# Respacing the hand-written order of an encoder layer's token mixer on one Trainium2 core

## The chip, the core and the metric

One core of one Trainium2 chip runs the whole layer as one program. The metric is the device time of one execution in microseconds (us); the median of several runs is compared. Engines are named as in the profile: PE (matmul), PEld (its weight loads), DVE (VectorE), ACT (ScalarE), POOL (GpSimd), SP (SyncE, which here only issues DMAs).

## What is computed

An encoder layer of 256 tokens with 1024 channels, all in float32:

```python
y = token_mixer(x)             # dilated-window attention (8 heads) and differential attention (4 heads),
                               # merged by sigmoid gates, then one output projection
x = layer_norm(alpha * x + y)
y = moe_ffn(x)                 # 32 experts, the 4 largest router logits of a token
x = layer_norm(alpha * x + y)

merged = sigmoid(g_a) * (o_a @ w_proj_a) + sigmoid(g_b) * (o_b @ w_proj_b)
token_mixer = merged @ w_out + b_out
expert(xb) = clamped_swiglu(xb @ w_up[e] + b_up[e]) @ w_down[e] + b_down[e]
```

## The kernel before

**Two halves.** The mixer (lines 131 to 700) reads 28 slabs of weights of 1 MB each (`w_mix`), the experts' half (784 to 959) reads 384 tiles of 1 MB each (`w_ex`, 12 for each expert). Expert tiles go through 20 named places in on-chip memory (`SLOTS`, line 81); the mixer uses the same places for its own data, and an expert tile can be fetched into a place as soon as the mixer's last use of it is over. `load()` (115) issues the next tile; the order of places is a0, qa, qb, tab, v, pt, p, gbc, oa, ob, ga, bup, gb, s0, s1, s2, w0, w1, x0, x1. All these DMAs go out on SP, which works through its list in order: a DMA that must wait for its place holds up those behind it.

**Pieces.** The mixer's matmuls go by 112 pieces of 512 columns, four in a slab. Float32 weights are split into a high and a low half: `split(n)` (176) lets ACT round the high half, and DVE or POOL subtract it to give the low half (line 187; POOL takes pieces 1 and 3 of a slab, except in slabs 2, 3, 8 and 9, which DVE does by line 184). The halves lie in a ring of four pieces (places w0, w1), so a split runs at most some three pieces ahead of PE. After the last split of a slab, its place is refilled with the slab three further on. `next_piece(n)` (199) first runs the hooks set for piece n-1, then `split(n+3)`; the caller then issues the matmuls of piece n, six or eight of them (lines 216 to 230).

**The order by hand.** `at(n, f)` (196) puts step f ahead of piece n+1. All engines run their own list in this order, with no scheduler. Lines 506 to 529 set it: attention A (dilated) for four head pairs as `tables_a`, `scores`, `scaled_a`, `turned_a`, `values_a`; attention B (differential) for four heads as the same steps with `_b`; `squares_b` and `subln_b` (its norm); `gate_sigmoids` (456); `bias_loads` and eight `bias_part` (432 to 448), in which POOL cuts the experts' up bias into three bfloat16 parts stacked in 96 rows (`bupp`), six or seven operations at a time; `residual_in` (453), alpha * x + b_out on DVE, from `x_loads`; `router_parts` (467), which folds the norm's gain into the router's weights through PE and DVE; and the `load`s. Units of 4 or 8 pieces follow one another (530): values, queries and keys of A are pieces 0 to 23, of B 24 to 47, gates 48 to 79, the two projections 80 to 95, the output projection 96 to 111. A unit ends with its results being read from PSUM by ACT or DVE (263 to 274); `n` in `unit(n)` times four is its first piece.

**The end of the mixer** (656 to 697) does the last quarter of the output projection for token tile 0, then 1 (`quarter(tt, i)`), with norm, transposes (`turned_x`), router logits and the choice of experts (`largest`) among them. Then the first expert's tokens are gathered (716) and its first matmuls run (742), which begin to set places free.

## Time and profile before

| | us |
|---|---|
| median of 3 runs (1165.01 to 1166.2) | 1166.2 |
| the profiled execution | 1164.82 |
| its span, first to last instruction | 1163.1 |
| PE busy | 1088.7 |
| DVE busy | 264.6 |
| ACT busy | 244.2 |
| POOL busy | 109.7 |

A busy PE is one with a matmul in flight; matmuls overlap, so a busy PE is not PE at its peak. In the timeline a row gives start, duration, engine, line, operation, written<-read tiles and count, and in brackets the idle time of the engine before it and the instruction that ended it. HBM traffic is 438 MB, of which the experts' tiles are 403 MB.

### The profile page before, as it was taken

How to read it: one execution, taken by the hardware profiler on the slowest of the kernel's cores; microseconds unless marked ns; L12 is line 12 of the kernel's file. 1: busy time of each engine (PE TensorE's matmuls, PEld its weight loads, DVE VectorE, ACT ScalarE, POOL GpSimd, SP SyncE). 2: the span in 40 equal slices, each digit the busy share in tenths (PEclk: the TensorE clock that was granted, in tenths of full speed). 3: DMA queues.
4: the chain of work that ended last, by engine and by line, in shares of the span. 5: the costliest groups of instructions: out<-in, count | busy, mean ns of one | idle time of the engine just before them, and what ended most of it. 6: DMA issues, size and time to landing. Idle time of an engine off the chain costs nothing.

```text
span 1163.1 us, 13105 instructions
## 1 busy us (share of the span) xinstructions
PE 1088.7 (94%) x5295; PEld 482.5 (41%) x5296; DVE 264.6 (23%) x512; ACT 244.2 (21%) x517; POOL 109.7 (9%) x114
## 2 busy tenths in 40 slices
PE   7999979899999999999999989999999899999994
PEld 6777758633434333333333323343433332323231
DVE  5675647311111111111111101111111111010113
ACT  5766644411111111111111101010111010101010
POOL 1535666000000000000000000000000000000000
PEclk9999999899999999999999989999999999999997
DMA  9663667799999999999999999999999999999992
GB/s 342 237 208 110 242 243 304 301 413 422 421 421 421 422 420 421 421 421 421 421 421 421 422 421 422 422 421 422 421 421 422 421 421 420 421 421 421 422 420 107
DMA packets 63542, 440.14 MB, mean 378 GB/s; under 512 B 7283, under 2 KB 8947, under 8 KB 10772
## 3 DMA queue, kind: packets, MB, share of 16 engines
q1 hardware_dynamic: 63138, 438.81, 92.1%
q8 instruction: 44, 0.72, 0.3%
q10 hardware_dynamic: 338, 0.43, 0.1%
q14 instruction: 22, 0.18, 0.0%
HBM read 438.17 MB, written 1.05 MB: 378 GB/s over the span
## 4 chain that ended last, share of the span: by engine, by line
DMA 54%; PE 37%; DVE 3%; POOL 2%; ACT 2%; issue 1%; SPq 0%; ACTq 0%; POOLq 0%; DVEq 0%
DMA r_ob<-in_w_ex 13%; DMA r_w<-in_w_ex 12%; DMA r_qa<-in_w_ex 12%; DMA r_s<-in_w_ex 9%; PE pu L742 8%; DMA r_pt<-in_w_ex 7%; PE pg L742 6%; PE pd L774 5%; PE acc L782 2%; PE px L716 2%; PE pt L219 2%; PE pt L229 2%; PE pt L230 1%; PE pt L228 1%; PE pt L220 1%
## 5 line engine op out<-in xcount | busy, mean ns | idle before, releaser
L731 DVE COPY ot<-po 128x256 f32<-128x256 f32 x32 | 13.6, 425 | 487.4 <-PE po L729 487.4
L720 ACT ACTIVATE xe<-px,bcol 128x128 f32<-128x128 f32 x128 | 48.1, 456 | 353.4 <-PE px L716 353.4
L939 POOL TENSOR_TENSOR r_pt<-r_pt,r_v 128x512 f32<-128x512 f32 x1 | 1.3, 1261 | 944.6 <-ACT r_pt L938 944.6
L750 DVE TENSOR_SCALAR gc<-pg 128x512 f32<-128x512 f32 x32 | 22.1, 692 | 249.8 <-PE pg L742 249.8
L716 PEld LDWEIGHTS px<-oh,x 128*128 128x128 f32 x512 | 61.6, 197 | 27.7 <-issue 12.4
L187 POOL TENSOR_TENSOR r_w<-r_s,r_w 128x512 fp32r<-128x512 f32 x46 | 64.5, 1412 | 86.6 <-ACT r_w L186 83.5
L716 PE MATMUL px<-oh,x 128*128 128x128 f32 x512 | 67.1, 287 | 0.9 <-DVE oh L706 0.8
L186 ACT CAST r_w<-r_s 128x512 fp32r<-128x512 f32 x96 | 57.3, 617 | 35.5 <-PE pt L230 23.2
L782 PE MATMUL acc<-y,ot 64*128 64x512 f32 x256 | 63.6, 615 | 0.7 <-ACT y L777 0.7
L777 ACT COPY y<-pd 128x512 f32<-128x512 f32 x32 | 18.7, 585 | 210.1 <-PE pd L774 210.1
L187 DVE TENSOR_TENSOR r_w<-r_s,r_w 128x512 fp32r<-128x512 f32 x50 | 46.7, 939 | 46.0 <-ACT r_w L186 45.7
L228 PE MATMUL pt<-r_w,r_x 128*128 128x512 f32 x112 | 46.9, 419 | 7.5 <-ACT r_w L186 7.5
L767 ACT COPY at<-pa 128x512 f32<-128x512 f32 x32 | 18.7, 585 | 160.7 <-PE pa L765 160.7
L229 PE MATMUL pt<-r_w,r_x 128*128 128x512 f32 x112 | 46.1, 412 | 2.7 <-POOL r_w L187 2.0
L230 PE MATMUL pt<-r_w,r_x 128*128 128x512 f32 x112 | 44.9, 401 | 0.0
L774 PE MATMUL pd<-r_s,at 128*64 128x512 f32 x168 | 38.7, 597 | 3.8 <-DMA r_s<-in_w_ex 3.8
L219 PE MATMUL pt<-r_x,r_w 128*128 128x512 f32 x112 | 41.3, 405 | 0.0
L782 PEld LDWEIGHTS acc<-y,ot 64*128 64x128 f32 x256 | 22.1, 186 | 41.8 <-issue 40.2
L742 PE MATMUL pu<-r_s,xe 128*64 128x512 f32 x144 | 35.4, 605 | 1.7 <-DMA r_s<-in_w_ex 1.7
L752 ACT ACTIVATE sg<-gc 128x512 f32<-128x512 f32 x32 | 20.1, 629 | 65.1 <-DVE gc L750 65.1
L742 PE MATMUL pg<-r_s,xe 128*64 128x512 f32 x144 | 33.4, 599 | 0.0
L220 PE MATMUL pt<-r_x,r_w 128*128 128x256 f32 x112 | 31.5, 281 | 0.0
(306 smaller groups left out, 1581.6 us busy)
## 6 DMA issues: line engine op xcount, KB each, us to landing
r_s<-in_w_ex SPq DMA_DIRECT2D x57, 1024.0 KB, 19.8
r_w<-in_w_ex SPq DMA_DIRECT2D x38, 1024.0 KB, 19.8
r_x<-in_w_ex SPq DMA_DIRECT2D x38, 1024.0 KB, 19.8
r_s<-in_w_mix SPq DMA_DIRECT2D x27, 1024.0 KB, 5.1
r_a<-in_w_ex SPq DMA_DIRECT2D x20, 1024.0 KB, 19.8
r_qa<-in_w_ex SPq DMA_DIRECT2D x20, 1024.0 KB, 19.8
r_qb<-in_w_ex SPq DMA_DIRECT2D x20, 1024.0 KB, 19.8
r_tab<-in_w_ex SPq DMA_DIRECT2D x19, 1024.0 KB, 19.8
```

The source lines that it names most:

```text
L186: S.copy(h, src)
L187: (G if i % 2 and m else V).tensor_sub(l, src, h.bitcast(F32))
L219: PE.matmul(os[j], h, x2, start=i == 0 and a == 0, stop=False)
L220: PE.matmul(os[j][:, :T], l, x2[:, :T], start=False, stop=False)
L228: PE.matmul(os[tt], h, w[:, :512], start=k == 0, stop=False)
L229: PE.matmul(os[tt], h, w[:, 512:], start=False, stop=False)
L230: PE.matmul(os[tt], l, w[:, :512], start=False, stop=k == last)
L716: PE.matmul(px[:, k], x1[:, tt, (4 * h + k) * P:(4 * h + k + 1) * P], oh[:, tt].rearrange("p a b -> p (a b)"), start=tt == 0, stop=tt == N ...
L720: S.activation(xe[:, 4 * h + k], px[:, k], AF.Identity, bias=bcol[:, f + 8:f + 9], scale=bcol[:, f:f + 1])
L742: PE.matmul(pu[h * CAP:(h + 1) * CAP], xe[:, k, i * CAP:(i + 1) * CAP], w(k)[:, h * 512:(h + 1) * 512], start=False, stop=k == KD - 1)
L774: PE.matmul(pd[dh * CAP:(dh + 1) * CAP], at[:, k % 4, k // 4 * CAP:(k // 4 + 1) * CAP], w(k)[:, dh * 512:(dh + 1) * 512], start=k == 0, st ...
L782: PE.matmul(o, ot[q, tt], y[q], start=start, stop=stop)
```

## The change

The steps stay the same in what they compute; their places and their cut change.

- **Attention** A: the five steps of a head pair start six pieces apart instead of five, turning and values one piece later; B starts three or four pieces later, its norm four later.
- **Bias**: the up bias lies in four groups of 32 rows (128 rows, the second group deselected by zeros in `sel`), so a part takes five POOL operations instead of six or seven; each of the 40 is a hook of its own, one at every second piece from 48 and one at every piece from 72. The bias matmul contracts 128 rows instead of 96.
- **Splits**: from slab 18 on, piece 1 of a slab goes to DVE instead of POOL.
- **Residual**: `x` and `b_out` are fetched at hook 2 instead of 13 and 5, and combined at hooks 11 and 14 instead of 66 and 67.
- **Sigmoids** of the third gate unit move from the unit's end into `gate_sigmoids`, which moves from hook 71 to 76.
- **Router's weights** in three steps at hooks 80, 82, 84 instead of one at 75.
- **Expert tiles**: hooks 39, 63, 64, 69, 70, 75, 82, 93, 95, 97, 99, 101 become 41, 67, 67, 73, 73, 76, 82, 93, 97, 99, 107 (the last one follows after the mixer's list).
- **End of the mixer**: tile 0's transposes and logits come one quarter earlier among the quarters of tile 1.

```diff
--- before.py
+++ after.py
@@ -94,8 +94,8 @@
     V.memset(ones, 1.0)
     epsc = const.tile([P, 1], F32, name="epsc")
     V.memset(epsc, EPS)
-    sel = const.tile([3 * NE, NE], BF16, name="sel")
-    bupp = const.tile([3 * NE, 2 * FE], BF16, name="bupp")
+    sel = const.tile([P, NE], BF16, name="sel")
+    bupp = const.tile([P, 2 * FE], BF16, name="bupp")
     x1 = const.tile([P, NT, D], F32, name="x1")
     posm = const.tile([P, NT, NE], F32, name="posm")
     gat = const.tile([P, NT, NE], F32, name="gat")
@@ -184,7 +184,7 @@
                 V.scalar_tensor_tensor(l, src, -0.125, h.bitcast(F32), op0=ALU.mult, op1=ALU.subtract)
             else:
                 S.copy(h, src)
-                (G if i % 2 and m else V).tensor_sub(l, src, h.bitcast(F32))
+                (G if i == 3 and m or i == 1 and 0 < m < 18 else V).tensor_sub(l, src, h.bitcast(F32))
             pieces_in[n] = w
             if i == 3 and m + 3 < 28:
                 load_slab(m + 3)
@@ -263,7 +263,7 @@
                     f = (n - 12) * 256
                     g = gates[f // 1024][:, i, f % 1024:f % 1024 + 512]
                     V.tensor_add(g, pt[i], gbc[:, f:f + 512])
-                    if n >= 16:
+                    if n >= 18:
                         S.activation(g, g, AF.Sigmoid)
                 elif c == 0:
                     V.tensor_add(v[:, i, b * 512:b * 512 + 512], pt[i], vbc[:, b])
@@ -408,11 +408,13 @@
             nc.sync.dma_start(trif, cst[:, C_TRI:C_TRI + P])
             nc.sync.dma_start(io1, cst[:, C_IO:C_IO + P])
             nc.sync.dma_start(sums, cst[:, C_SEL:])
+
+        def x_loads():
+            for tt in range(NT):
+                nc.sync.dma_start(xs[:, tt], x[tt * P:(tt + 1) * P])
             nc.sync.dma_start(bo, bcast(b_out, P, D))
 
-        def x_loads():
-            for tt in range(NT):
-                nc.sync.dma_start(xs[:, tt], x[tt * P:(tt + 1) * P])
+        def gate_rows():
             nc.sync.dma_start(gbc, bcast(b_in[3072:5120], P, 2048))
 
         def lambdas():
@@ -427,25 +429,26 @@
 
 
 
-        bup = slot("bup")[:3 * NE]
+        bup = slot("bup")
+        bias_ops = []
 
         def bias_loads():
-            for i in range(3):
-                nc.sync.dma_start(bup[i * NE:(i + 1) * NE], b_up)
-
-        def bias_part(m):
-            c = slice(m * 256, (m + 1) * 256)
-            if m < 3:
-                q = slice(m * NE, (m + 1) * NE)
-                G.tensor_copy(sel[q], ident[q, q])
-            G.tensor_copy(bupp[:, c], bup[:, c])
-            G.tensor_sub(bup[:, c], bup[:, c], bupp[:, c])
-            for i in range(1, 3):
+            G.memset(sel[NE:2 * NE], 0.0)
+            for i in range(4):
                 q = slice(i * NE, (i + 1) * NE)
-                G.tensor_copy(bupp[q, c], bup[q, c])
-            q = slice(2 * NE, 3 * NE)
-            G.tensor_sub(bup[q, c], bup[q, c], bupp[q, c])
-            G.tensor_copy(bupp[q, c], bup[q, c])
+                nc.sync.dma_start(bup[q], b_up)
+                if i != 1:
+                    G.tensor_copy(sel[q], ident[q, q])
+            for m in range(8):
+                c = slice(m * 256, (m + 1) * 256)
+                bias_ops.append(lambda c=c: G.tensor_copy(bupp[:, c], bup[:, c]))
+                for h in (slice(2 * NE, P), slice(3 * NE, P)):
+                    bias_ops.append(lambda c=c, h=h: G.tensor_sub(bup[h, c], bup[h, c], bupp[h, c]))
+                    bias_ops.append(lambda c=c, h=h: G.tensor_copy(bupp[h, c], bup[h, c]))
+
+        def bias_op():
+            if bias_ops:
+                bias_ops.pop(0)()
 
         xs = x1
         bo = moe.tile([P, D], F32, name="bo", tag="xe0")
@@ -455,6 +458,7 @@
 
         def gate_sigmoids():
             S.activation(gates[0], gates[0], AF.Sigmoid)
+            S.activation(gates[1][:, :, 0:512], gates[1][:, :, 0:512], AF.Sigmoid)
 
         wrg = const.tile([P, KD, NE], F32, name="wrg")
         sums = const.tile([P, NE], F32, name="sums")
@@ -464,21 +468,26 @@
         ones16 = const.tile([P, P], BF16, name="ones16")
         tri16 = const.tile([P, P], BF16, name="tri16")
 
-        def router_parts():
-
-            G.tensor_copy(ones16, ones)
-            G.tensor_copy(tri16, trif)
-            V.tensor_mul(wrg, wr, bcol[:, 41:49, None].to_broadcast([P, KD, NE]))
-            pl = pst.tile([P, 512], F32, name="pt", tag="tp")
-            PE.matmul(pl[:, 128:384], ones, wrg.rearrange("p a b -> p (a b)"), start=True, stop=True)
-            V.tensor_reduce(csm, pl[:, 128:384].rearrange("p (a b) -> p b a", a=KD), axis=mybir.AxisListType.X, op=ALU.add)
-            V.tensor_scalar(csm, csm, -1.0 / D, None, op0=ALU.mult)
-            V.tensor_add(wrg, wrg, csm[:, None].to_broadcast([P, KD, NE]))
-            for k in range(KD):
-                PE.matmul(pl[:1, :NE], bcol[:, 49 + k:50 + k], wr[:, k], start=k == 0, stop=k == KD - 1)
-            V.tensor_add(lgb, pl[:1, :NE], brr)
-            PE.matmul(pl[:, 64:64 + NE], ones[0:1], lgb, start=True, stop=True)
-            V.tensor_copy(lgbb, pl[:, 64:64 + NE])
+
+        def router_parts(i):
+            if i == 0:
+                G.tensor_copy(ones16, ones)
+                G.tensor_copy(tri16, trif)
+                V.tensor_mul(wrg, wr, bcol[:, 41:49, None].to_broadcast([P, KD, NE]))
+            elif i == 1:
+                pl = pst.tile([P, 512], F32, name="pt", tag="tp")
+                PE.matmul(pl[:, 128:384], ones, wrg.rearrange("p a b -> p (a b)"), start=True, stop=True)
+                for k in range(KD):
+                    PE.matmul(pl[:1, :NE], bcol[:, 49 + k:50 + k], wr[:, k], start=k == 0, stop=k == KD - 1)
+                V.tensor_reduce(csm, pl[:, 128:384].rearrange("p (a b) -> p b a", a=KD), axis=mybir.AxisListType.X,
+                                op=ALU.add)
+                V.tensor_scalar(csm, csm, -1.0 / D, None, op0=ALU.mult)
+                V.tensor_add(wrg, wrg, csm[:, None].to_broadcast([P, KD, NE]))
+                V.tensor_add(lgb, pl[:1, :NE], brr)
+            else:
+                pl = pst.tile([P, 512], F32, name="pt", tag="tp")
+                PE.matmul(pl[:, 64:64 + NE], ones[0:1], lgb, start=True, stop=True)
+                V.tensor_copy(lgbb, pl[:, 64:64 + NE])
 
         nlam = const.tile([P, 1], F32, name="nlam")
         def x_parts(k):
@@ -508,25 +517,26 @@
         at(1, small_loads)
         at(5, more_loads)
         at(9, load)
-        at(13, x_loads)
+        at(2, x_loads)
+        at(13, gate_rows)
+        at(11, residual_in, 0)
+        at(14, residual_in, 1)
         at(20, lambdas)
         for i in range(4):
-            for n, f in ((17, tables_a), (21, lambda i: scores(0, i)), (24, scaled_a), (26, turned_a), (28, values_a)):
+            for n, f in ((17, tables_a), (21, lambda i: scores(0, i)), (24, scaled_a), (27, turned_a), (29, values_a)):
+                at(n + 6 * i, f, i)
+            for n, f in ((46, table_b), (49, lambda i: scores(1, i)), (52, scaled_b), (54, turned_b), (56, values_b)):
                 at(n + 5 * i, f, i)
-            for n, f in ((43, table_b), (45, lambda i: scores(1, i)), (48, scaled_b), (50, turned_b), (52, values_b)):
-                at(n + 5 * i, f, i)
-        at(39, load)
         at(34, bias_loads)
-        for i in range(8):
-            at(46 + 7 * i, bias_part, i)
-        for n in (63, 64, 69, 70, 75, 82, 93, 95, 97, 99, 101):
+        for n in [*range(48, 72, 2), *range(72, 108)]:
+            at(n, bias_op)
+        for n in (41, 67, 67, 73, 73, 76, 82, 93, 97, 99, 107):
             at(n, load)
-        at(69, squares_b)
-        at(71, subln_b)
-        at(71, gate_sigmoids)
-        at(66, residual_in, 0)
-        at(67, residual_in, 1)
-        at(75, router_parts)
+        at(73, squares_b)
+        at(75, subln_b)
+        at(76, gate_sigmoids)
+        for i in range(3):
+            at(80 + 2 * i, router_parts, i)
         for n in range(20):
             if n < 12 and n % 6 > 1 or n % 2 == 0:
                 unit(n)
@@ -671,11 +681,11 @@
         summed(3, 0, py)
         stats(0)
         quarter(1, 0)
-        quarter(1, 1)
         turned_x(3, 0, xTs[3])
         normed(0)
+        quarter(1, 1)
+        logits(3, 0, xTs[3])
         quarter(1, 2)
-        logits(3, 0, xTs[3])
         largest(0)
         quarter(1, 3)
         summed(3, 1, py)
@@ -837,7 +847,7 @@
 
         def bias_of(e):
             def bias(o, c):
-                PE.matmul(o, sel[:, e:e + 1].to_broadcast([3 * NE, CAP]), bupp[:, c:c + 512], start=True, stop=False)
+                PE.matmul(o, sel[:, e:e + 1].to_broadcast([P, CAP]), bupp[:, c:c + 512], start=True, stop=False)
             return bias
 
         xes, ohs, ots, ys, acts = {}, {}, {}, {}, {}
```

## Rows read from the trace of the kernel before

**Rows 1.** Windows: us; PE, PEld, DVE, ACT, POOL busy (count), PE clock, DMA share, GB/s.

```profile
205.00:209.00 4.00, 4.00 (x38) 3.67 (x37) 2.21 (x5) 1.78 (x4) 1.44 (x2) 1.00 0.02 6
...
226.00:232.00 6.00, 6.00 (x32) 2.02 (x32) 1.31 (x7) 3.41 (x8) 0.00 (x0) 1.00 0.77 288
232.00:1130.00 898.00, 859.05 (x4102) 310.99 (x4098) 119.33 (x211) 105.12 (x219) 0.00 (x0) 0.99 1.01 421
```

**Rows 2.** Timeline of SP: start, duration, issue of expert tiles around the mixer's end.

```profile
208.92 1.29 SPq L123 DMA_DIRECT2D r_s<-in_w_ex  x3
...
228.24 0.33 SPq L123 DMA_DIRECT2D r_a<-in_w_ex  x1
```

**Rows 3.** Windows, as in Rows 1, of the mixer after its start.

```profile
145.00:156.00 11.00, 7.39 (x38) 4.62 (x37) 6.68 (x9) 5.11 (x7) 7.60 (x11) 0.84 0.83 328
20.00:209.00 189.00, 179.73 (x956) 141.85 (x955) 117.89 (x233) 114.74 (x249) 103.60 (x105) 0.99 0.61 226
```

**Rows 4.** Timeline of PE: matmuls of the mixer that waited.

```profile
50.23 0.66 PE L328 MATMUL pt<-ident,r_p 128*128 128x128 f32 x4 [0.62 <-DVE r_p L336]
...
60.30 0.50 PE L229 MATMUL pt<-r_w,r_x 128*128 128x512 f32 x1 [1.18 <-POOL r_w L187]
...
99.49 0.55 PE L328 MATMUL pt<-ident,r_p 128*128 128x128 f32 x3 [0.48 <-DVE r_p L359]
...
147.98 0.50 PE L228 MATMUL pt<-r_w,r_x 128*128 128x512 f32 x1 [1.02 <-ACT r_w L186]
149.33 0.65 PE L229 MATMUL pt<-r_w,r_x 128*128 128x512 f32 x1 [0.85 <-POOL r_w L187]
...
152.19 1.03 PE L473 MATMUL pt<-wrg,ones 128*128 128x256 f32 x2 [0.50 <-DVE wrg L471]
153.74 0.63 PE L478 MATMUL pt<-wr,bcol 128*1 128x32 f32 x16 [0.52 <-DVE csm L474]
155.08 0.41 PE L480 MATMUL pt<-lgb,ones 1*128 1x32 f32 x2 [0.72 <-DVE lgb L479]
...
170.68 0.50 PE L229 MATMUL pt<-r_w,r_ob 128*128 128x512 f32 x1 [2.48 <-POOL r_w L187]
```

**Rows 5.** Timeline of POOL: mask additions, a bias part's first operation, splits.

```profile
45.74 3.00 POOL L294 TENSOR_TENSOR r_pt<-r_pt,r_tab 128x512 f32<-128x512 f32 x2
48.70 2.60 POOL L187 TENSOR_TENSOR r_w<-r_s,r_w 128x512 fp32r<-128x512 f32 x2
...
164.88 0.86 POOL L441 CAST bupp<-r_bup 96x256 bf16<-96x256 f32 x1
...
169.04 2.83 POOL L187 TENSOR_TENSOR r_w<-r_s,r_w 128x512 fp32r<-128x512 f32 x2
```

**Rows 6.** Timeline of ACT: tables of attention A, and the sigmoids.

```profile
44.32 1.15 ACT L293 ACTIVATE r_pt<-r_tab 128x512 f32<-128x512 f32 x2
...
140.01 1.28 ACT L267 ACT_TABLE_LOAD   x1
...
144.56 1.05 ACT L390 CAST r_ob<-ob 128x1024 fp32r<-128x1024 f32 x1 [1.35 <-DVE ob L388]
145.52 1.91 ACT L457 ACTIVATE r_ga<-r_ga 128x2048 f32<-128x2048 f32 x1
```

**Rows 7.** Timeline of DVE: a residual operation, and splits beside POOL and alone.

```profile
130.97 1.21 DVE L454 SCALAR_TENSOR_TENSOR x<-x,bo 128x1024 f32<-128x1024 f32 x1
132.11 1.76 DVE L187 TENSOR_TENSOR r_w<-r_s,r_w 128x512 fp32r<-128x512 f32 x1
...
160.50 0.69 DVE L187 TENSOR_TENSOR r_w<-r_s,r_w 128x512 fp32r<-128x512 f32 x1 [2.05 <-ACT r_w L186]
```

**Rows 8.** Slab 4: issue (SP), KB and us to landing (DMA issues), first split (ACT).

```profile
17.85 0.33 SPq L147 DMA_DIRECT2D r_s<-in_w_mix  x1
...
r_s<-in_w_mix SPq DMA_DIRECT2D x1, 1024.0 KB, 6.3
...
27.28 0.62 ACT L186 CAST r_w<-r_s 128x512 fp32r<-128x512 f32 x1 [0.30 <-PE pt L219]
```

More of the change, by code (lines that the diff above doesn't have):

```diff
@@ L410, in more_loads @@
             nc.sync.dma_start(sums, cst[:, C_SEL:])
-            nc.sync.dma_start(bo, bcast(b_out, P, D))
         def x_loads():
@@ L415, in x_loads @@
                 nc.sync.dma_start(xs[:, tt], x[tt * P:(tt + 1) * P])
+            nc.sync.dma_start(bo, bcast(b_out, P, D))
+        def gate_rows():
             nc.sync.dma_start(gbc, bcast(b_in[3072:5120], P, 2048))
```

## The prediction

> **What bounds the kernel now.** I read the windows first. From 232 to 1130 us the DMA engines are never idle and move 421 GB/s [rows 1]; a tile of 1.049 MB so takes 2.49 us, and PE's share of work matters nowhere in that stretch. So the end is the moment at which this stream becomes continuous, plus what is left to fetch. SP's timeline gives that moment: the places s0 to s2 are refilled at 208.92, as soon as the last slab is split, and a0, freed by the first expert's first matmuls, at 228.24 [rows 2]. In between seven tiles go out (s0 to s2, w0, w1, x0, x1), 7 x 2.49 = 17.4 us of transfer in 19.3 us. From 228.24, 384 - 20 = 364 tiles remain, 364 x 2.49 = 906 us; 228 + 906 = 1134, and some 29 us of last expert, norm and output make the span of 1163.1 (1164.82 for the execution).
>
> Two things follow. Between 205 and 209 the DMA share is 0.02 [rows 1]: all that could be fetched has been, and the stream waits for the mixer's last split. So a microsecond taken from the mixer ahead of 208.9 shifts the whole stream and the end by a microsecond, whatever the loads do, while all 13 earlier tiles are still in by then. What is gained between 208.9 and 228.2 counts for less: at 226 to 232 the share is 0.77 [rows 1], 1.4 us of idle DMA, so the seven tiles would become the limit after about that.
>
> Inside the mixer PE sets the pace: from 20 to 209 us it is busy 179.73 of 189 us [rows 3], and the rest are waits that the timeline of PE names [rows 4]. Matmuls of a piece start 0.23 us apart but last 0.39, so a wait costs what stands in brackets and about 0.15 us more.
>
> **The change part by part.** *Bias.* At 164.88 POOL begins a bias part, which holds it until 169.04, 4.2 us for six operations; the two splits behind it come late, and PE waits 2.48 us at 170.68 [rows 4, 5]. After the change at most one such operation (0.86 us at most here, nearer 0.4 to 0.7 in the average of this part) stands ahead of a split that has three pieces, some 4 us, of lead: -2.6 us. Smaller waits for POOL make up most of the 0.9 us that the rows leave of the 9.3 idle us (rows 4 and 0.9 are all of it): half of them, -0.5. The 40th operation falls on hook 99; place bup is fetched behind it, at about 196 us, while four tiles are queued ahead of it, so this costs nothing; were POOL 10 us late, each further one would delay the last tiles. Four row groups instead of three are one 256 KB fetch more in a stretch with idle DMA, and a bias matmul of 128 rows instead of 96 has the same columns: nothing.
>
> *Attention A.* PE waits 1.18 us at 60.30 for a POOL split behind mask additions whose tables ACT could not make before the scores one hook earlier. With six pieces a period the tables come two hooks behind the scores, and the next split after them is in slab 8, which POOL has no part in: -1.3. The wait of 0.62 at 50.23 (scaling too near turning) goes too, with one piece more of lead: -0.75 [rows 4]. But something moves the other way. The second pair's tables move from hook 22 to 23, and turning and scores, which stood ahead of piece 27 and gave its split time, move to hook 27, behind it. ACT made those tables at 44.32 [rows 6]; it will get to them after one more split and the unit's two reads from PSUM, about 45.8; POOL's two additions of 3.00 us together [rows 5] then end at 49.4 and the low half of piece 27, 1.3 us (half of the two in 2.60), at 50.7. PE stood at the end of piece 26 at 48.95 (50.23 less 0.62 and less the first half of the turning, 0.66) and 0.3 us sooner now, so it wants that half at about 48.6: +2.1. Bounds: 0 if ACT gets to the tables first, +2.1; I take the upper end, as each term has its row. At B the same distances remain; of 0.48 us at 99.49 I take half back, since POOL no longer works through a bias part just then: -0.3.
>
> *Sigmoids.* In the trace ACT rounds ob at 144.56 (1.05), does the first gate's sigmoid at 145.52 (1.91) and only then the split of piece 75; the table load of 1.28 us lies earlier, at 140.01, under the third unit's sigmoids [rows 6]. PE waits 1.02 and 0.85 us [rows 4]. Afterwards the burst is one piece later but longer. Behind the rounding come a split (0.62), the table load (1.28, exposed now, since no sigmoid comes ahead), 1.91, half as much again for the third unit (1.0) and the split of piece 80 (0.62): 5.4 us. The rounding ends 2.8 us after PE's norm matmuls, as now, so the high half is there after 8.2 and the low one after 8.9; PE has pieces 76 to 79, 4 x 1.37 = 5.5 us. New wait 3.2 against 1.87 + 0.3 now: +1.0. The measure that the reckoning is sound: by it the split of piece 75 is 1.0 late now, as the row has it. Bounds: 0 and +3. The Trainium skill, "ScalarE: Activation LUTs", What ACT_TABLE_LOAD costs, gives about 1.28 us for the load and 1.38 for a drain behind it at each switch; by that the burst would be 1.4 us longer and the sum 1.4 smaller. The load itself agrees with the row.
>
> *Router.* Three waits of 0.50, 0.52 and 0.72 us stand in one chain of PE and DVE [rows 4]. In three steps two pieces apart each DVE result has 2.7 us: -1.74 - 0.45 + 0.2 = -2.0 (0.2 for what I may have missed). Over 145 to 156 the granted clock is 0.84 [rows 3], so a third of that stretch, 3.5 us, ran at 1.2 GHz; I put its cost at 1.0. After it one wait of 3 us stands there instead of five short ones; whether the clock falls again I leave even: -0.2.
>
> *Residual.* The two operations of 1.21 us [rows 7] leave a full DVE at 131 to 135, where PE does not wait: nothing. At hooks 11 and 14 DVE has a split of 0.69 and little else per piece. Their loads are dearer: 1.5 MB now stand ahead of slab 4, 3.7 us at 421 GB/s. Slab 4 is issued at 17.85 and split from 27.28 on [rows 8]; PE wants it three pieces later, at about 31.4. The queue is full there and takes 6.3 us to land it, at 24.2, so it would land at about 28.0, the split be over at 29.4: 2 us to spare. I take 0; the bound is +2 if broadcast rows move at half the rate. Slabs 5 and 6 have more room.
>
> *Splits to DVE.* Ten splits of 1.3 us leave POOL and cost DVE 0.69 alone, up to 1.76 beside POOL [rows 7]; DVE is busy 118 of 189 us [rows 3]: nothing.
>
> *Expert tiles.* v and pt go out four pieces later and share a place in the list with slab 22, which has nine pieces of lead; the DMA share over 20 to 209 is 0.61 [rows 3]: nothing. *End of the mixer.* Tile 0 gains a quarter (0.7 us), but tile 1 ends the chain: 0, bounds -0.5 and +0.5.
>
> **Sum:** -2.6 - 0.5 - 1.3 - 0.75 + 2.1 - 0.3 + 1.0 - 2.0 - 0.2 = -4.55, call it -4.5. The profiled execution gives 1164.8 - 4.5 = 1160.3; the runs' median is 1.4 above it, 1161.7. I forecast 1160.5.
>
> **The rivals.** *More is won* (0.2): neither new wait shows, as ACT's lists run further ahead than I reckon; then +2.1, +1.0 and 0.8 for the clock fall out of the sum: -8.5, 1155 to 1158. *Nothing is won* (0.18): the sigmoids take their upper bound, the clock is low behind them, slab 4 comes late; -4.5 + 2 + 1 + 1.5 = 0, 1163.9 to 1167. That the single operations do not help is part of it: should POOL's queue stay full anyhow, 2.6 is lost, 1163. *Slower* (0.06): DVE is held by POOL. A split takes DVE 0.69 alone and 1.76 beside POOL [rows 7]. With one operation at every piece, 28 of them from hook 72 on, and ten more splits on DVE, each piece could cost it 0.4 us more; once its work per piece passes the 1.37 us of PE, PE follows it: 28 x 0.4 = 11 us less the gain of 4.5, 1171. Against it: DVE's mean is 0.62 of the time with POOL's bursts in it, and POOL has less work after the change. The Trainium skill, "SBUF — State Buffer", SBUF: two separate sides, calls the port that the two share an exclusive lock held for a whole instruction, which blocks the other; the row of 1.76 agrees, and by it cutting bursts up removes no blocking.
>
> **How the numbers follow.** Forecast 0.56: 1158 to 1163.5, from the bounds of the sigmoids and of the tables. A measurement of this kernel can tell about 0.2% from no change, 2.3 us: under 1163.9 is faster, over 1168.5 slower. Forecast and the first rival are faster, with a small part of the second: 0.77; same 0.17; slower 0.06. Eight in ten lie between 1155 and 1165.
>
> **What would show it.** Right: no wait of PE over 1 us for POOL around pieces 31 and 85, no waits for wrg, csm or lgb; s0 refilled 4 to 5 us earlier than 208.9, the DMA share before it still near 0, the stream unchanged behind it. A wait of about 2 us at piece 27 and of about 3 us at piece 80. Wrong: a wait for slab 4, a stream that starts no earlier, or matmuls waiting for DVE all over pieces 72 to 100.

## The result, and the profile after

Four runs of the changed kernel have a median of 1157.9 us (1157.5 to 1159.3), four of the kernel before beside them 1165.8 (1165.0 to 1166.2). The ratio is 0.9923 [0.991, 0.9936]: 7.9 us by the medians, 9.0 by the ratio. The forecast of 1160.5 lies 2.6 us above it, its range of 1155 to 1165 holds it. The profiled execution of after, 1159.26 us, is the slowest of its four, while that of before, 1164.82, is the fastest of its own; so the two traces differ by 5.6 us only, and the rest has to be looked for in a second pair (below).

The page of after, span and busy time:

```profile
span 1157.5 us, 13104 instructions
...
PE 1087.1 (94%) x5295; PEld 483.8 (42%) x5296; DVE 271.8 (23%) x522; ACT 244.9 (21%) x516; POOL 94.6 (8%) x97
```

PE does the same work as before, POOL 15 us less. Windows of after (columns as in [rows 1]):

```profile
143.00:183.00 40.00, 37.51 (x183) 29.97 (x183) 25.65 (x41) 22.75 (x34) 22.24 (x30) 0.96 0.67 251
20.00:204.50 184.50, 178.20 (x959) 143.01 (x958) 125.28 (x243) 115.45 (x249) 88.40 (x88) 0.99 0.63 233
201.00:204.50 3.50, 3.50 (x34) 3.17 (x33) 2.21 (x5) 1.53 (x4) 1.29 (x1) 1.00 0.00 0
...
222.00:227.00 5.00, 5.00 (x28) 1.57 (x26) 1.31 (x7) 2.31 (x6) 0.00 (x0) 1.00 0.91 327
227.00:1122.00 895.00, 857.18 (x4092) 311.02 (x4088) 119.35 (x211) 105.41 (x219) 0.00 (x0) 0.99 1.01 421
```

Timeline of SP in after, the refill of s0 to s2 and of a0:

```profile
204.47 1.28 SPq L123 DMA_DIRECT2D r_s<-in_w_ex  x3
...
222.96 0.33 SPq L123 DMA_DIRECT2D r_a<-in_w_ex  x1
```

Beside [rows 1 to 3]: the stream still waits for the mixer's last split (DMA share 0.00 ahead of 204.5) and afterwards still moves 421 GB/s. Nearly the whole difference of the spans, 5.6 us, is there when a0 is refilled: s0 is 4.45 us earlier, a0 5.28. PE's first matmul starts at 6.43 us in before and at 6.76 in after, so the mixer itself is 4.8 us shorter. PE's idle time from 20 us to s0 fell from 9.27 us to 184.50 - 178.20 = 6.30, so 3.0 of the 4.8 us are idle time; the rest lies in matmuls that count as busy (lost overlap behind waits, and the clock, below).

Timeline of PE in after: the matmuls that waited longest ahead of s0 (idle time and what ended it in brackets), and in the last row one behind it.

```profile
46.90 0.50 PE L229 MATMUL pt<-r_w,r_x 128*128 128x512 f32 x1 [0.48 <-POOL r_w L187]
...
51.26 0.50 PE L229 MATMUL pt<-r_w,r_x 128*128 128x512 f32 x1 [1.35 <-POOL r_w L187]
...
111.05 1.10 PE L369 MATMUL pv<-r_pt,r_v 128*128 128x256 f32 x4 [1.65 <-DVE r_ga L265]
...
153.56 0.50 PE L229 MATMUL pt<-r_w,r_x 128*128 128x512 f32 x1 [0.88 <-POOL r_w L187]
...
156.38 0.50 PE L228 MATMUL pt<-r_w,r_oa 128*128 128x512 f32 x1 [1.39 <-ACT r_w L186]
...
157.10 0.61 PE L229 MATMUL pt<-r_w,r_oa 128*128 128x512 f32 x1 [0.22 <-DVE r_w L187]
...
211.69 0.44 PE L586 MATMUL pt<-ident,x 128*128 128x128 f32 x2 [0.52 <-DVE x L602]
```

Of [rows 4] the waits of 2.48 us (bias), 1.18 (tables), 0.62 (turning) and the router's three are gone. So are the 1.02 and 0.85 at piece 75. In their place stand 1.35 at piece 27 and 0.88, 1.39 and 0.22 at pieces 79 and 80, where the prediction looked for new ones, and 0.48 at piece 25 and 1.65 at piece 57, where it did not.

The wait at piece 27: ACT's tables and POOL's queue in after. Timeline of ACT, then of POOL:

```profile
46.63 1.15 ACT L293 ACTIVATE r_pt<-r_tab 128x512 f32<-128x512 f32 x2
```

```profile
47.34 2.60 POOL L294 TENSOR_TENSOR r_pt<-r_pt,r_tab 128x512 f32<-128x512 f32 x2 [0.49 <-ACT r_pt L293]
49.90 3.00 POOL L187 TENSOR_TENSOR r_w<-r_s,r_w 128x512 fp32r<-128x512 f32 x2
```

POOL waits 0.49 us for the tables, adds the masks for 2.6 us, and only then makes the low half that PE's row at 51.26 takes. The wait at pieces 79 and 80, timeline of ACT in after:

```profile
150.07 1.05 ACT L390 CAST r_ob<-ob 128x1024 fp32r<-128x1024 f32 x1 [4.23 <-DVE ob L388]
151.03 0.62 ACT L186 CAST r_w<-r_s 128x512 fp32r<-128x512 f32 x1
151.66 1.28 ACT L460 ACT_TABLE_LOAD   x1
152.96 1.92 ACT L460 ACTIVATE r_ga<-r_ga 128x2048 f32<-128x2048 f32 x1
154.78 1.04 ACT L461 ACTIVATE r_gb<-r_gb 128x1024 f32<-128x1024 f32 x1
155.72 1.65 ACT L186 CAST r_w<-r_s 128x512 fp32r<-128x512 f32 x3
```

Rounding, split, table load and two sigmoids stand one behind the other as in the prediction; the split of piece 80 begins at 155.72, and PE, out of pieces, starts at 156.38. And the wait that was not foreseen, timeline of DVE in after:

```profile
109.10 0.18 DVE L319 RECIPROCAL rz<-z 128x4 f32<-128x4 f32 x1 [1.12 <-ACT r_p L316]
109.61 0.69 DVE L187 TENSOR_TENSOR r_w<-r_s,r_w 128x512 fp32r<-128x512 f32 x1 [0.33 <-ACT r_w L186]
110.22 1.28 DVE L265 TENSOR_TENSOR r_ga<-pt,r_gbc 128x512 f32<-128x512 f32 x2
```

`values_b(0)` at hook 56 now comes right behind the end of a gate unit (pieces 48 to 55). It needs a PSUM buffer that DVE reads out at line 265, and these reads stand in DVE's list behind a split and the softmax's reciprocal, which itself waited 1.12 us for ACT's exponentials.

### The profile page after: what moved, and what is told of

It is laid out like the page before. It is cut to its first block, busy times and chain, and to the rows that moved or that the text cites. A ratio compares the mean times of both kernels' runs of the same rounds, so it can differ in the third digit from the quotient of the medians.

```text
span 1157.5 us, 13104 instructions
## 1 busy us (share of the span) xinstructions
PE 1087.1 (94%) x5295; PEld 483.8 (42%) x5296; DVE 271.8 (23%) x522; ACT 244.9 (21%) x516; POOL 94.6 (8%) x97
## 3 DMA queue, kind: packets, MB, share of 16 engines
HBM read 438.43 MB, written 1.05 MB: 380 GB/s over the span
## 4 chain that ended last, share of the span: by engine, by line
PE 50%; DMA 44%; DVE 2%; issue 1%; ACT 1%; POOL 1%; SPq 0%; ACTq 0%; DVEq 0%; POOLq 0%
DMA r_w<-in_w_ex 10%; PE pu L752 10%; PE pg L752 9%; DMA r_pt<-in_w_ex 9%; DMA r_ob<-in_w_ex 9%; DMA r_qa<-in_w_ex 9%; PE pd L784 8%; DMA r_s<-in_w_ex 7%; PE px L726 3%; PE acc L792 3%; PE pt L228 2%; PE pt L229 2%; PE pt L230 2%; PE pt L219 2%; PE pt L220 1%
## 5 line engine op out<-in xcount | busy, mean ns | idle before, releaser
L187 DVE TENSOR_TENSOR r_w<-r_s,r_w 128x512 fp32r<-128x512 f32 x60 | 53.2, 897 | 36.3 <-ACT r_w L186 35.8
L187 POOL TENSOR_TENSOR r_w<-r_s,r_w 128x512 fp32r<-128x512 f32 x36 | 51.2, 1427 | 100.9 <-ACT r_w L186 83.7
```

The lines of the kernel that those rows point to most:

```text
L187: (G if i == 3 and m or i == 1 and 0 < m < 18 else V).tensor_sub(l, src, h.bitcast(F32))
```

## The experiments

The theory: taking the bias part's burst and the router's chain apart made the gain; attention's new spacing and the sigmoids take a little back; residual, tiles and end weigh nothing. The first rival: the respacing of attention is what won. The second, formed when one part alone won more than its waits: PE's clock. In the table s0 and a0 are the moments of their refill in the trace, ratios are against the kernel before on the same chip.

| kernel | median us | ratio | s0 | a0 | span |
|---|---|---|---|---|---|
| before, first trace | 1165.8 | 1 | 208.92 | 228.24 | 1163.1 |
| before, second trace | 1167.5 (one) | | 212.92 | 232.76 | 1165.7 |
| after, first trace | 1157.9 | 0.9923 | 204.47 | 222.96 | 1157.5 |
| after, second trace | 1157.8 (one) | | 203.51 | 223.12 | 1156.0 |
| before + bias | 1163.0 | 0.9966 [0.9952, 0.9979] | 208.54 | 228.41 | 1160.7 |
| before + router | 1160.5 | 0.9951 [0.9938, 0.9965] | 206.67 | 225.48 | 1158.4 |
| before + bias + router | 1158.0 | 0.9925 [0.9912, 0.9938] | 203.07 | 221.89 | 1154.7 |
| before + residual | 1167.9 | 1.0007 [0.9998, 1.0016] | 212.89 | 232.19 | 1164.8 |
| before + useless matmuls | 1165.4 | 0.9987 [0.9978, 0.9996] | 210.54 | 229.36 | 1164.1 |
| after, old attention | 1158.1 | 0.9925 [0.9911, 0.9938] | 204.91 | 223.45 | 1156.1 |
| after, old end | 1158.4 | 0.9923 [0.9908, 0.9937] | 204.61 | 223.43 | 1158.3 |
| after, three steps moved | 1155.7 | 0.9914 [0.99, 0.9927] | 201.63 | 220.19 | 1153.4 |
| the same, more moved | 1155.5 | 0.9905 [0.9892, 0.9918] | 201.88 | 220.42 | 1152.8 |
| the same, sigmoids behind 80 | 1152.1 | 0.9876 [0.9861, 0.9891] | 196.68 | 215.24 | 1148.3 |

In every one of these traces 932 to 935 us lie between a0's refill and the end of the span. So a microsecond of the mixer is a microsecond of the whole, in every variant. The difference within these bounds belongs to the execution and not to the kernel: it is 934.9 and 932.9 us in the two traces of before, 934.5 and 932.9 in those of after. PE's first matmul too starts anywhere from 6.2 to 7.4 us and moves s0 with it. So single traces are compared from the first matmul to s0, and times by the ratio.

### The bias work alone, on before

```diff
+        for n in [*range(48, 72, 2), *range(72, 108)]:
+            at(n, bias_op)
-        for i in range(8):
-            at(46 + 7 * i, bias_part, i)
```

With it go the four row groups, as in the change.

> The kernel before with one edit: the 40 bias operations of POOL each in a hook of its own, on 128 rows (the places of all other steps as before; place bup is fetched one hook later). Theory: POOL's splits no longer stand behind a burst, so the wait of 2.48 us at piece 85 and the two smaller ones of 0.33 and 0.11 at pieces 91 and 98 go, with 0.15 us each of lost overlap: 2.9 to 3.4 us faster than before, about 1162.6 us. The wait of 1.18 us at piece 31 stays, since it comes from attention's tables. Rival (DVE is held at every piece by POOL's single operations): no wait named POOL at piece 85, but waits of PE for DVE's low halves over pieces 72 to 100, and 1166 us or more.

Measured: 1163.0, 0.9966, which is 4.0 us. The wait of 2.48 us at piece 85 is gone. In the table s0 is only 0.4 us earlier than in before's first trace; but the clock is low for longer here (mean 0.87 from 143 to 183 us, against 0.96), and against before's second trace, which also has 0.87, it is 4.4 us earlier. One wait is new; timeline of PE, then of POOL:

```profile
116.40 0.50 PE L229 MATMUL pt<-r_w,r_x 128*128 128x512 f32 x1 [0.90 <-POOL r_w L187]
```

```profile
115.08 1.27 POOL L187 TENSOR_TENSOR r_w<-r_s,r_w 128x512 fp32r<-128x512 f32 x1 [3.75 <-issue]
```

No single operation held this split: POOL stood idle for 3.75 us ahead of it. It began when ACT's rounding was over, which started at 114.35, 0.43 us later than in before, behind a softmax of attention B. Ahead of that, a split on DVE took 1.40 us beside an operation of POOL, where before has 0.92; that this made the wait is not shown.

So the term of the bias work was right in kind and 0.9 short (3.1 forecast, both its parts).

### The router's three steps alone, on before

```diff
-        at(75, router_parts)
+        for i in range(3):
+            at(75 + 2 * i, router_parts, i)
```

> The kernel before with one edit: the router's weights in three steps at hooks 75, 77 and 79 instead of in one at 75. Theory: the chain of PE and DVE (waits of 0.50, 0.52 and 0.72 us) goes, 1.74 us and 0.45 of lost overlap, and a part of the lower clock behind it: 2.0 to 3.0 us faster than before, 1163 to 1164 us. Rival (the burst of sigmoids just ahead is what holds this stretch; ACT's splits are late anyhow and PE waits for them in place of the router's chain): less than 1 us, 1165 us or more.

Measured: 1160.5, 0.9951, which is 5.7 us, twice what was expected. Its own waits of 1.74 us are gone, the waits for the sigmoids stayed, and of the 2.48 for POOL there are 0.86 at 158.36 and the row below, piece 85, in the timeline of PE:

```profile
168.46 0.50 PE L229 MATMUL pt<-r_w,r_ob 128*128 128x512 f32 x1 [1.05 <-POOL r_w L187]
```

That makes 1.74 + 2.48 - 0.86 - 1.05 = 2.3 us; PE's idle time from 20 us to 205 falls nearly as much, from 9.27 to 7.06. From the first matmul to s0 this trace is 3.0 us shorter than before's first and 6.9 shorter than its second; the 5.7 measured lies between. What differs besides the waits is the clock. Windows of this kernel, then of before (the second row is used further down):

```profile
143.00:183.00 40.00, 35.86 (x174) 27.93 (x173) 25.20 (x36) 21.46 (x33) 27.83 (x31) 1.00 0.67 257
```

```profile
143.00:183.00 40.00, 33.69 (x155) 25.75 (x153) 22.43 (x33) 19.39 (x31) 25.51 (x30) 0.96 0.65 244
20.00:196.00 176.00, 166.73 (x856) 130.09 (x855) 110.69 (x217) 109.22 (x238) 98.33 (x101) 0.99 0.61 223
```

The granted clock of the 40 us is 1.00 against 0.96, all of it at 2.4 GHz against a part at 1.2.

### Bias and router together, on before

The two edits above, and the change's rule for splits.

> The kernel before with three edits: POOL's bias operations in single hooks, the router's weights in three steps (hooks 75, 77, 79), and piece 1 of slabs 18 to 27 split by DVE. Attention, norm, sigmoids, residual, the places of most tiles and the end stand as before. Theory: these edits are the whole gain of the change; s0 is refilled at about 205 (208.92 before, 204.47 in the changed kernel) and the time is that of the changed kernel, 1157 to 1159.5 us. Rival (the wider spacing, the early residual or the end carry a part of their own): over 1160.5 us, s0 after 206.

Measured: 1158.0, 0.9925, which is 8.8 us and the same as the whole change within the intervals. s0 is refilled at 203.07, where 205 was expected.

The two parts alone gave 4.0 + 5.7 = 9.7, so they nearly add up. All that remains of the change is worth nothing in sum, within the 1.5 us that the intervals leave.

### The old attention and sigmoids in after

```diff
-            for n, f in ((17, tables_a), (21, lambda i: scores(0, i)), (24, scaled_a), (27, turned_a), (29, values_a)):
-                at(n + 6 * i, f, i)
+            for n, f in ((17, tables_a), (21, lambda i: scores(0, i)), (24, scaled_a), (26, turned_a), (28, values_a)):
+                at(n + 5 * i, f, i)
...
-        at(76, gate_sigmoids)
+        at(71, gate_sigmoids)
```

B's steps, its norm and the third unit's sigmoids go back as well.

> The changed kernel with one part undone: attention, its norm and the sigmoids stand at the hooks of before (periods of five pieces, sigmoids of the third gate unit at that unit's end), all else is as changed. Theory: the respacing of attention costs more waits than it takes away (new: 0.49 at piece 25, 1.35 at 27, 0.21 at 54, 1.65 at 57, 0.88 at 79, 1.39 and 0.22 at 80, 6.2 us together; gone: 0.14, 0.62, 1.18, 0.56, 0.15, 1.02 and 0.85, 4.5 together), so this is 1.5 to 2 us faster than the changed kernel, about 1156.2 us. Rival (the wider spacing is what made the gain): the old waits come back in full and more, 1160 us or above.

Measured: 1158.1, 0.9925: neither. It is as fast as after, so the respacing, with the sigmoids, neither won nor lost more than the intervals leave, some 1.5 us. PE stands idle for 5.85 us from 20 to 205 us, against 6.30 in after: what the new spacing removes it makes elsewhere. The wait of 0.49 at piece 25, which the expectation counts among attention's, stays here: it is not attention's (next run).

### The residual's early loads alone, on before

```diff
+        at(2, x_loads)
+        at(13, gate_rows)
+        at(11, residual_in, 0)
+        at(14, residual_in, 1)
-        at(66, residual_in, 0)
-        at(67, residual_in, 1)
```

> The kernel before with one edit: x and b_out fetched at hook 2, combined at hooks 11 and 14. Theory: the two DVE operations at 131 to 135 us kept nobody waiting, and slab 4 lands about 4 us later yet in time: no change, 1165 to 1168 us, s0 refilled within 0.7 us of 208.92, no wait of PE for slab 4 between 25 and 40 us. Rival (DVE is full where the two operations stood, and its splits and reads profit): s0 1 us or more earlier and the wait of 1.02 us at piece 75 shorter.

Measured: 1.0007 [0.9998, 1.0016], no change, and no wait between 24 and 44 us, where slab 4 would be late. But the wait at piece 25 is here, which no kernel without the early loads has; timeline of PE:

```profile
46.38 0.50 PE L229 MATMUL pt<-r_w,r_x 128*128 128x512 f32 x1 [0.46 <-POOL r_w L187]
```

The softmax of the first head pair starts on DVE at 41.91 instead of 41.36, and the splits of slab 6 come behind it; what holds DVE there is not shown. So the residual's term is not quite nothing, though the times cannot tell 0.5 us. s0 was expected within 0.7 us of 208.92 and stood at 212.89: a miss, which raised the question of the clock. Windows of this kernel:

```profile
143.00:183.00 40.00, 34.31 (x138) 26.08 (x137) 19.51 (x28) 16.68 (x26) 21.84 (x25) 0.83 0.54 207
```

### Both kernels again, unchanged

> The kernel before, unchanged, profiled once more. In its first profile the granted clock over 145 to 165 us is low for 3.4 us; in two kernels that leave the router's chain as it was (bias alone, residual alone) it is low for 10.2 us there. Theory: the length of that spell is chance from run to run, long as a rule, and its price explains why the runs of before have a median 1 to 2 us above the profiled one: mean clock over 145 to 165 us at or below 0.80, s0 refilled at 210 to 213. Rival (the spell belongs to the edits): 0.91 and 208.9 again.

> The changed kernel, unchanged, profiled once more. Theory: its start of the stream depends less on chance: s0 refilled within 0.7 us of 204.47, waits of 1.35, 1.65, 0.88 and 1.39 us as in the first profile, the clock over 145 to 165 us low for 3.4 us or not at all. Rival: s0 elsewhere by more than 1 us.

Windows and SP of before, second trace:

```profile
143.00:183.00 40.00, 33.06 (x136) 25.39 (x136) 19.69 (x29) 17.25 (x27) 21.28 (x25) 0.87 0.59 223
```

```profile
212.92 1.28 SPq L123 DMA_DIRECT2D r_s<-in_w_ex  x3
```

Windows and SP of after, second trace:

```profile
143.00:183.00 40.00, 37.31 (x189) 29.77 (x189) 28.43 (x42) 23.40 (x35) 22.84 (x31) 1.00 0.67 257
```

```profile
203.51 1.28 SPq L123 DMA_DIRECT2D r_s<-in_w_ex  x3
```

Before came out as its theory had it (s0 at 212.92; mean clock 0.83 over 145 to 165 us, where 0.80 or less was expected). After did not quite: its s0 is 0.96 us earlier than in the first trace, where 0.7 was the bound. The larger waits are those of the first traces but for one: before has 1.03, 0.85, 1.45 and 2.47 us among them, where the first trace has 1.02, 0.85, 0.50 and 2.48; after has 1.36, 1.65, 0.88 and 1.37. And the clock differs. The time at 1.2 GHz in these 40 us follows from the mean, as 1.2 is half of 2.4: 40 x 2 x (1 - mean), so 3.2 us in the first trace of before and 10.4 in the second.

What that costs depends on where it lies. Timeline of PE in before, first trace (start of pieces 76 and 80), then second:

```profile
155.41 0.50 PE L228 MATMUL pt<-r_w,r_x 128*128 128x512 f32 x1
...
161.01 0.39 PE L228 MATMUL pt<-r_w,r_oa 128*128 128x512 f32 x1
```

```profile
148.47 0.50 PE L228 MATMUL pt<-r_w,r_x 128*128 128x512 f32 x1 [1.03 <-ACT r_w L186]
...
152.69 0.67 PE L473 MATMUL pt<-wrg,ones 128*128 128x256 f32 x2 [1.45 <-DVE wrg L471]
...
155.69 0.80 PE L228 MATMUL pt<-r_w,r_x 128*128 128x512 f32 x1
156.28 0.63 PE L229 MATMUL pt<-r_w,r_x 128*128 128x512 f32 x1
156.71 0.63 PE L230 MATMUL pt<-r_w,r_x 128*128 128x512 f32 x1
...
163.99 0.39 PE L228 MATMUL pt<-r_w,r_oa 128*128 128x512 f32 x1
```

In the first trace the low stretch lies ahead of piece 76, between the waits for ACT, POOL and DVE, and is almost hidden by them: from piece 75 (147.98 [rows 4]) to piece 76 it takes 7.43 us, in the second trace, at 1.00 there until near its end, 7.22. So the 3.2 us cost some 0.2. In the second trace it lies behind them, where PE waits for nothing: matmuls start 0.43 us apart there instead of 0.23, which is 0.47 us lost for each us. From piece 75 to piece 80 it takes 15.52 us against 13.03, and from there to s0 48.93 against 47.91, with a second low stretch behind the wait at piece 85, where the first trace has none: 3.5 us for 7.2, or 0.49 each. (The other 0.5 of the 4.0 us at s0 is there ahead of piece 75.) In after's first trace the 3.2 us lie behind the wait at piece 80. Its second trace, at 1.00, has that wait here, in the timeline of PE:

```profile
156.42 0.49 PE L228 MATMUL pt<-r_w,r_oa 128*128 128x512 f32 x1 [1.37 <-ACT r_w L186]
```

From it to s0 the first trace takes 48.09 us and the second 47.09: the low clock cost 1.0 there. From the first matmul to s0 the first pair differs by 4.8 us and the second by 206.41 - 197.15 = 9.3. The clock's share taken out, both leave the same: 4.8 - 0.2 + 1.0 = 5.6 and 9.3 - 3.7 = 5.6. That is what the waits and the overlap lost behind them are worth.

The mean clock of a whole run is 0.984 over the 41 runs of before that stand beside the experiments, 0.986 in the five of after, 0.984 with the bias work alone, 0.986 with the router alone, 0.988 with both, 0.983 with the residual alone. It cannot be priced in this way: a part of the low clock lies in the experts' stream (0.98 to 0.99 between 600 and 1140 us in both kernels), where DMA sets the pace with a share of 1.00 to 1.01, and a straight line through the 41 runs of before gives only some 0.14 us of span for each us at the lower clock.

### Filling PE's waits with useless matmuls, on before

```diff
+                    if n + i == 75 and tt == 0:
+                        fill(3)
...
+            fill(2)
             PE.matmul(pl[:, 128:384], ones, wrg.rearrange("p a b -> p (a b)"), start=True, stop=True)
...
+        at(74, fill, 4)
```

`fill(c)` puts c matmuls of 512 columns into PE's list whose result nobody reads; two and three more stand ahead of the router's other matmuls.

> The kernel before with matmuls of no use (512 columns each, their result is never read) put where PE waits at piece 75 and in the router's chain: four ahead of piece 75, three behind its first matmul, two, two and three ahead of the router's three groups. Nothing else is moved, so the engines that PE waits for finish when they did; the waits are filled rather than shortened. Theory: the low clock behind these waits is a cost of its own, 2 to 4 us in a run as they mostly are; with the gaps filled the clock stays at 2.4 GHz, over 145 to 165 us its mean is 1.00, and the time falls by 2 to 3.5 us, to 1163.5 to 1165 us. Rival (the low clock is hidden behind the waits, which last as long anyhow): 1166 us or more.

Measured: 1165.4, 0.9987 [0.9978, 0.9996], a gain of 1.5 us with work added, less than the 2 to 3.5 expected. Windows, and the timeline of PE at piece 85:

```profile
143.00:168.00 25.00, 23.66 (x116) 18.12 (x114) 13.39 (x20) 13.45 (x21) 13.43 (x17) 1.00 0.66 248
...
143.00:183.00 40.00, 36.18 (x167) 28.15 (x166) 20.85 (x31) 18.84 (x31) 23.94 (x29) 0.96 0.65 246
```

```profile
170.84 0.80 PE L239 MATMUL pt<-r_w,r_ob 128*128 128x512 f32 x1 [2.48 <-POOL r_w L187]
```

The clock stayed at 1.00 in the stretch that was filled, and fell behind the wait that was not, where a single matmul takes 0.80 us. The waits themselves are no shorter: up to there this trace runs some 0.4 us behind before's first, and piece 75 starts at 148.38 against 147.98, the router's first matmul at 152.62 against 152.19. So the clock has a price of its own, shown at 1.5 us; the rest of the estimate is not shown, since the fall was only put off.

### The old order of the end in after

```diff
+        quarter(1, 1)
         turned_x(3, 0, xTs[3])
         normed(0)
-        quarter(1, 1)
-        logits(3, 0, xTs[3])
         quarter(1, 2)
+        logits(3, 0, xTs[3])
```

> The changed kernel with the order of the last quarters as before (transposes, norm and logits of token tile 0 one quarter later). Theory: tile 1 ends the chain, so at most its wait for DVE before the last transposes moves, 0.82 instead of 0.52 us: from the refill of s0 to that of a0 18.8 us instead of 18.5, and the time is that of the changed kernel within 0.5 us. Rival (the earlier quarter is worth its 0.7 us of PE): 0.7 us or more between the two refills, 1158.6 us or above.

Measured: 1158.4, 0.9923, the same; from s0 to a0 18.82 us against 18.49. PE waits 0.82 us for DVE ahead of the last transposes, as expected, where after waits 0.52.

### Three steps of after moved, then more, then the sigmoids

```diff
+                at(22 if f is tables_a and i == 1 else n + 6 * i, f, i)
...
+                at(57 if f is values_b and i == 0 else n + 5 * i, f, i)
...
-        at(76, gate_sigmoids)
+        for i in range(3):
+            at(76 + i, gate_sigmoids, i)
```

> The changed kernel with its three largest new waits taken away by the place of a step: the second pair's tables one hook earlier (22), the first values of attention B one hook later (57), the sigmoids in three operations at hooks 76, 77 and 78. Theory: the mixer sets the start of the stream, so each wait is worth its full length: 1.35 + 1.65 and about 1.6 of the 2.5 at pieces 79 and 80, with 0.15 us each of lost overlap: 4.5 to 5 us faster than the changed kernel, 1153 us. Rival (the stream of tiles is the limit by now, or the cover of one wait only hides the next): 1156 to 1158 us with the waits gone from the trace.

Measured: 1155.7, 0.9914, below the rival's range but far nearer to it than to the theory's 1153; s0 is 2.8 us earlier than in after's first trace, 1.9 than in its second, the ratio only 1 us better and the median 2.2, where 4.5 to 5 were expected. The wait at piece 57 is down to 0.27, so its cause was read rightly. The other two moves only shortened or shifted theirs; timeline of PE, piece 27, and 0.88 at piece 79 stays:

```profile
50.92 0.50 PE L229 MATMUL pt<-r_w,r_x 128*128 128x512 f32 x1 [0.79 <-POOL r_w L187]
```

Next, slab 6 split by DVE alone, the rounding of ob in a hook of its own (76), the sigmoids at 77 to 79, the router at 82, 85 and 88:

```diff
-                (G if i == 3 and m or i == 1 and 0 < m < 18 else V).tensor_sub(l, src, h.bitcast(F32))
+                (G if m != 6 and (i == 3 and m or i == 1 and 0 < m < 18) else V).tensor_sub(l, src, h.bitcast(F32))
...
+        at(76, rounded_b)
         for i in range(3):
-            at(76 + i, gate_sigmoids, i)
+            at(77 + i, gate_sigmoids, i)
```

> The changed kernel with its new waits worked on further: tables, values and sigmoids as in the run that moved these three (sigmoids at hooks 77 to 79), and besides slab 6 split by DVE alone (POOL is busy with the tables of attention A there), the rounding of ob in a hook of its own (76, behind one more split), and the router's steps at hooks 82, 85 and 88. Theory: the waits of that run at pieces 25 to 27 (1.4 us), 79 and 80 (1.0) and for the router's chain (0.7) go for the most part; s0 is refilled 2 us earlier than there (201.63), at about 199.6, and the time is 1153 to 1154 us. Rival (each step that moves pushes another wait ahead of it): s0 at 201 or later, 1155 to 1156 us.

Measured: 1155.5, 0.9905, which is the rival's forecast. The waits at pieces 25 to 27 and the router's are gone, but not the time; timeline of PE:

```profile
157.19 0.50 PE L228 MATMUL pt<-r_w,r_oa 128*128 128x512 f32 x1 [1.91 <-ACT r_w L186]
...
158.59 0.50 PE L229 MATMUL pt<-r_w,r_oa 128*128 128x512 f32 x1 [0.90 <-POOL r_w L187]
```

ACT's burst has only gone on to the next pieces. Last, the same sigmoids behind those of the fourth gate unit, whose table load they share:

```diff
         for i in range(3):
-            at(77 + i, gate_sigmoids, i)
+            at((80, 81, 83)[i], gate_sigmoids, i)
...
-        at(81, lambda: S.activation(dummy, gates[1][:, 1, 1023:1024], AF.Sqrt))
+        at(85, lambda: S.activation(dummy, gates[1][:, 1, 1023:1024], AF.Sqrt))
```

> The run with the further moves (a_best), with the three gate sigmoids at hooks 80, 81 and 83, behind the fourth unit's own sigmoids, whose wait for DVE covers the table load, and the norm's table load at hook 85 instead of 81. Theory: the waits of 1.91 and 0.90 us at piece 80 go, with at most 0.5 us new at 83: s0 at 199.3 (201.88 there), 2 to 2.5 us faster, 1153 us. Rival (the burst only moves on and PE meets it at piece 83 or 84): a wait of 1.5 us or more there, 1155 us or above.

Measured: 1152.1 (1150.3 to 1152.4), 0.9876 [0.9861, 0.9891], faster than both kernels and 3.4 us by the ratio better than the run before it. Windows and SP:

```profile
143.00:183.00 40.00, 40.00 (x205) 32.71 (x204) 31.92 (x49) 24.46 (x38) 26.31 (x33) 1.00 0.78 294
20.00:196.00 176.00, 175.30 (x951) 141.04 (x950) 123.98 (x244) 114.80 (x250) 84.59 (x86) 1.00 0.66 244
```

```profile
196.68 1.28 SPq L123 DMA_DIRECT2D r_s<-in_w_ex  x3
```

PE is busy 175.30 of 176 us, where before it was busy 166.73 in the same stretch. No wait over 0.3 us is left between 20 and 200 us, and the clock is 1.00. s0 is 5.2 us earlier than in the run before it, where 2.6 were expected: 2.8 us of idle time are gone, its first matmul starts 0.95 us sooner (6.41 against 7.36), and the clock between 143 and 183 us is 1.00 instead of 0.96.

## Why the prediction was right, and where it was off

**The bound** held in every trace: the stream is fixed to within the 2.6 us by which executions differ, and the mixer's microseconds count one for one. That the seven tiles would soon limit the stretch from s0 to a0 did not decide anything: the DMA share at its end rose from 0.77 [rows 1] to 0.91, and the stretch became 0.8 us shorter.

**The bias work** (-3.1): right. Alone it gave 4.0. The rival in which DVE is held by POOL's many operations did not occur: no matmul of after waits over 0.5 us for DVE between pieces 72 and 100, though DVE's busy time in the mixer grew from 117.89 us [rows 3] to 125.28.

**Attention** (-1.3, -0.75, +2.1, -0.3): both waits went, and the new one came where it was forecast, as 1.35 instead of 2.1. The step that failed is "At B the same distances remain": they do among B's steps, but not against the gate unit's end, and 1.65 us at piece 57 came of it. With it, attention's terms sum to some 1.0 lost where 0.25 was forecast to be won; the measurement with the old spacing can tell neither from nothing.

**Sigmoids** (+1.0): new wait 0.88 + 1.39 + 0.22 = 2.5 against 3.2 forecast, so some 0.3 instead of 1.0; the chain that was reckoned is the one in the trace. The sum without a drain behind the table load was the better one: the load of 1.28 us starts at 151.66 and the sigmoid at 152.96. The 1.38 us more that the Trainium skill gives in "ScalarE: Activation LUTs", What ACT_TABLE_LOAD costs, do not show in this row.

**Residual, splits, tiles, end** (0): right within what the times can tell, two of them measured alone. PE did not wait for slab 4. But the residual's early loads brought the 0.48 at piece 25, which the forecast does not have.

**Router and clock** (-2.0 and -0.2): the clock is the term that was mis-sized. The router's waits went as forecast. But the clock was taken from one trace of before, whose 3.5 us at 1.2 GHz were priced at 1.0, and whether it would fall again was left even. In that trace the low stretch cost only some 0.2, as it lay between waits; in before's second trace, with 10.4 us between 143 and 183, it cost 3.7; in after 1.0 or nothing. So the step that failed is to take one execution for the kernel: the clock is worth -0.8 in one pair (it costs more after the change) and 3.7 in the other. Without the clock the forecast for the waits is -4.35, and both pairs show -5.6. Between the two lie errors of both signs: 0.9 too little for the bias work, 0.7 too much for the sigmoids and 0.75 for the tables, 1.65 and 0.48 that were not forecast (the 4.0 of the bias work may hold some of the clock). These sum to -4.6, so 1.0 of the 5.6 no term accounts for. That a part of these errors cancelled is luck.

**What stays open.** The clock's share of the 7.9 to 9.0 us is bounded only: 1.5 us shown by filling the waits, some 2.3 to 3.4 by what the waits' 5.6 leave. What makes the low stretch 3.2 us in one execution and 10.4 in another of the same kernel no run here shows. Nor could the router's clock and its waits be separated in after itself.

## What to carry to other kernels

When a step is moved in a hand-written order, ask what it covered for the step behind it, and which buffer it takes that another engine must first read out: the larger waits that this change made came from these two. The last kernel gained 5.5 us over after (0.9876 against 0.9923), 3.4 of them by giving the burst of sigmoids a place where its table load and its wait were already paid for. A chain of short waits costs its brackets and, beside them, what the clock loses behind it. Read the clock of that stretch in two profiles of the unchanged kernel before it is priced, since nearly the same waits went with 3.2 us at the lower clock in one and 10.4 in the other; and ask whether the low stretch lies between waits, where 3.2 us cost 0.2, or among matmuls that wait for nothing, where each us cost some 0.5. Where the time seems to come from many small edits, one part at a time on the kernel before tells more than the difference of two traces: two parts, with the rule for splits, carried all of it within some 1.5 us.

## What the runs showed of the hardware

The clock's low stretch has a length that the kernel does not fix: unchanged, with nearly the same waits, before had a mean granted clock of 0.96 and of 0.87 between 143 and 183 us, and s0 4.0 us apart, 3.5 of it made in that stretch and behind it. At the lower clock matmuls of 512 columns started 0.43 us apart instead of 0.23. Matmuls that nobody reads kept the clock at 1.00 for the 25 us in which they filled the waits, and it fell at the next wait of 2.48 us instead. After a table load of 1.28 us ACT began its next function 0.02 us later.
